# Two blocks on one core: four gate pairs by seven products, input normalised once, low parts by adding transfers, scales with 128-partition operands

## The chip, the cores and the metric

The kernel runs on one core of one Trainium2 chip, in one launch. The metric is device microseconds (us) of that core, as a median of runs. All numbers are fp32 on the outside; inside, a product of two fp32 matrices is made of three TensorE matmuls on rounded operands (type fp32r): high·high, high·low and low·high, where "high" is the rounded number and "low" is what rounding left.

## The reference, cut to what matters

The input x has 512 tokens of width 1024. A first block (normalisation, one wide projection, three branches, an output projection, a residual and a normalisation) feeds a second block. The change lies mostly in the second.

```python
def rmsnorm(x, g):
    y = xf * lax.rsqrt(jnp.mean(xf * xf, axis=-1, keepdims=True) + EPS)
    return (y * g).astype(x.dtype)
...
def first_block(...):
    h = rmsnorm(x, norm_g[l]); proj = h @ w_in[l]
    ...
    x = x + jnp.concatenate([y_a, y_b, y_c], axis=-1) @ w_out[l]
    return rmsnorm(x, final_norm_g)
...
def second_block(x, ...):
    p = h @ w_in[l] + b_in[l]
    a_u, a_v, q, k, v, r, a_low, g_a, g_b = split(p)
    y_a = spatial_gating(a_u, a_v, ...)          # gelu(a_u) * (mixed layer_norm(gelu(a_v)))
    o = gla_chunked(q, k, v, log_f)
    o = o * lax.rsqrt(jnp.mean(jnp.square(o), axis=-1, keepdims=True) + LN_EPS)
    y_b = o * gla_norm_g[l] * silu(r)
    m = sigmoid(g_a) * y_a + sigmoid(g_b) * y_b
    h = layer_norm(DEEPNORM_ALPHA * h + m @ w_out[l], ln1_g[l], ln1_b[l])
    f = jnp.square(relu(h @ w_ff1[l])) @ w_ff2[l]
    return layer_norm(DEEPNORM_ALPHA * h + f, ln2_g[l], ln2_b[l])
```

## The kernel before, in words

**A recorder and a planner.** The kernel does not issue instructions as it is written. Every call (`tt`, `act`, `mm`, a DMA) is recorded by `Recorder.add`, and at the end `rec.order` (L326) puts all instructions of the five queues (PE, ACT, DVE, POOL, SP) into an order by a list scheduler with a cost for each instruction; `rec.issue` (L484) emits that order. Each queue then runs in order. This is why every instruction stands at L502 in the profile. Buffers are bounded: 64 pages of 128x512 (`pg`), 8 PSUM banks (`ps`), 4 raw weight slots (`wr`), 4 slots each for high (`wh`, `fh`) and low (`wl`, `fl`) parts of weights.

**Weights.** Weights come as 184 chunks, mostly of 512 KB (128x1024). `load_to` (L631) loads a chunk into a raw slot by SP's queue; `split_to` (L639) calls `split` (L560): ACT copies to the rounded high part, DVE subtracts it from the raw chunk for the low part. `run_ahead` (L698) keeps it two chunks ahead.

**Feature-major units** (`unit_fm`, L727). One unit makes 128 output features of all 512 tokens: 8 slices of the inner dimension, three matmuls each, 24 matmuls of 512 columns. The second block has 40 such units in the order of `ORDER2` (L508): first `au0` to `au7`, then q, k, r, ga and gb. Each is evacuated from PSUM by a DVE multiplication with the page `rh` (the reciprocal root mean square of each token, spread over 128 partitions), and then by ACT. The operand hh/hl is thus the input without its per-token scale.

**Token-major units** (`units_tok`, L812). `av` (L1467 ff.) and `v` (L1530 ff.) have tokens on the partitions; a group of two chunks gives 96 matmuls of 256 or 260 columns. Order before: av, v, then the 40 units.

**Pairs** (`pair_weights` L731, `pair_fast` L765, `fast_operands` L793). In the first feed-forward matrix 11 pairs of units are made by seven products of half size (a Strassen-Winograd scheme): 7 x 4 x 3 = 84 matmuls of 256 columns in place of 48 of 512. Their weights are sums of chunks, made and split on DVE and ACT in advance; they take all four `wh`/`wl` slots (called `fh`/`fl` there). Four banks are combined by DVE and ACT.

**Scales and side work.** A scale by token is a column per tile of 128 tokens. `rsqrt_cols` (L868) makes the reciprocal root: square root on ACT, then five small DVE instructions. To spread it over partitions, `rows_of` (L881) transposes the columns to rows in a 64-partition tile `bhl`, and `bcast` (L891) multiplies a 64x128 selection (`sel`) with it, 128 columns at a time. `scale_page`, `mlstm_end`, `gla_end`, `mm_shift` and `ln1` use this; `gates` uses `sel` with 512 columns. Side work (`sg`, `gla`, `gla_end`, `resid`, ...) are generators in lanes which the units step.

Of the kernel before, what the change touches and what calls it, by code (L numbers as in the profile page):

```python
# [8 lines left out]
F32 = mybir.dt.float32  # L9
# [13 lines left out]
SLOT = 1088  # L23

# [145 lines left out]
class Recorder:  # L170
# [54 lines left out]
    def costs(self, o):  # L225
# [20 lines left out]
        elif eng == "DVE":  # L246
# [10 lines left out]
            elif o.what == "copy_predicated":  # L257
                o.cost = 160 + 1.1 * n
            elif o.what == "tensor_tensor_scan":
                o.cost = 1200  # L260
            elif n <= 16:
                o.cost = 165
        elif eng == "POOL":
            o.port = o.what != "memset"
            o.cost = 190 + 2.15 * n
# [94 lines left out]
    def schedule(self, caps, prio):  # L360
# [74 lines left out]
        while done < n:  # L435
# [11 lines left out]
            if e == "SP":  # L447
                b = o.kw["out"]
                size = 4.0 * 128 * (b.n if isinstance(b, View) else 512)
                wire = max(wire, s + 500) + size / 250.0  # L450
                o.end = max(wire, s + cost) + 1500
# [19 lines left out]
            for j in o.users:  # L471
                u = ops[j]
                u.ready = max(u.ready, o.end if u.eng != e else s + cost + (0 if e != "SP" else o.end - s - cost))
# [41 lines left out]
def tile_two_blocks(ctx, tc, wa, wb, xT, memT, vec, cst, rows, poolw, wst, wg2, out):  # L515
# [71 lines left out]
    sel = rec.tile(per, [64, 16], F32R, name="sel")  # L587
    selc = rec.tile(per, [128, 4, 4], F32R, name="selc")
    eps6 = rec.tile(per, [128, 1], F32, name="eps6")
    eps5 = rec.tile(per, [128, 1], F32, name="eps5")  # L590
    one1 = rec.tile(per, [128, 1], F32, name="one1")
    warm = rec.tile(per, [128, 1], F32, name="warm")
    rsm = rec.tile(per, [128, 24], F32, name="rsm")
    bhl = [rec.tile(per, [64, 128], F32R, name=f"bhl{i}") for i in range(2)]
# [6 lines left out]
    chunks = "b" * 4 + "a" * (4 + 4 + 8 + 2 + 2 + 2 + 2 + 4 + 12) + "a" * 12 + "a" * 8 + "b" * 8 + "a" * (8 + 32 + 8 + 32 + 32)  # L601
# [13 lines left out]
    fast_ff = set(range(FF1 + 4, FF1 + 4 + 2 * NFAST))  # L615

# [22 lines left out]
    def split_to(i):  # L639
        while n_sp[0] <= min(i, NCH - 1):  # L640
# [10 lines left out]
            else:  # L651
# [3 lines left out]
                split(h, l, t)  # L655
# [137 lines left out]
    def fast_operands(x, xh, xl):  # L793
# [3 lines left out]
        for kk in range(4):  # L797
            j = kk + 4
            for m, (t, s) in {1: (kk, L), 2: (j, L), 3: (j, R)}.items():
                b[m][0][kk], b[m][1][kk] = xh[t][:, s], xl[t][:, s]  # L800
            t56, t74 = pg(), pg()
            tt(V, t56[:, L], x[kk][:, R], x[kk][:, L], ALU.subtract)
            tt(V, t56[:, R], x[j][:, R], t56[:, L], ALU.subtract)
            tt(V, t74[:, L], x[j][:, R], x[kk][:, R], ALU.subtract)
            tt(V, t74[:, R], x[j][:, L], t56[:, R], ALU.subtract)
# [56 lines left out]
    def sqrt_of(v, n):  # L862
        t = small(16)[:, 0:n]
        act(t, v, ACTF.Sqrt)
        yield
        return t

    def rsqrt_cols(dst, v, n, t=None):  # L868

        if t is None:  # L870
            t = small(16)[:, 0:n]
            act(t, v, ACTF.Sqrt)
# [6 lines left out]
    bsel = [0]  # L879

    def rows_of(cols, n):  # L881

        p = bank()
        PE.transpose(out=p[0:n, 0:128], in_=cols, identity=ident)
        b = bhl[bsel[0] % 2]
        bsel[0] += 1
        act(b[0:n], p[0:n, 0:128], ACTF.Copy)
        tt(V, b[32:32 + n], p[0:n, 0:128], f(b[0:n]), ALU.subtract)
        return b

    def bcast(out, b, i):  # L891
        mm(out, sel[:, i:i + 1].to_broadcast([64, 128]), b, True, True)
# [6 lines left out]
    if True:  # L899
# [5 lines left out]
        V.memset(one1, 1.0)  # L905
        V.tensor_copy(out=onesr, in_=ones)
        for b in bhl:
            G.memset(f(b), 0.0)
# [16 lines left out]
        for k in range(8):  # L925
# [5 lines left out]
            split(w[1][:, s], w[2][:, s], w[0][:, s], eng=G)  # L931
        V.tensor_copy(out=sel, in_=ct[0:64, C_SEL:C_SEL + 16])
        V.tensor_copy(out=selc, in_=ct[:, C_SELC:C_SELC + 16].rearrange("p (h c) -> p h c", h=4))
# [22 lines left out]
    def scale_cols(dst, acc, nt, n, eps, p=None):  # L956
# [3 lines left out]
        rsqrt_cols(dst, v, nt)  # L960

    def scale_page(key, cols, nt):
        b = rows_of(cols, nt)
        yield
        p = bank()
        for j in range(nt):
            bcast(p[:, j * 128:(j + 1) * 128], b, j)
# [41 lines left out]
    def gates():  # L1009
# [4 lines left out]
        yield  # L1014
        ig, fg, ab, b, m, keep = [pg() for _ in range(6)]
# [7 lines left out]
        G.memset(f(ahl[0:64]), 0.0)  # L1023
# [31 lines left out]
        for h in range(4):  # L1055
            p = bank()
            mm(p, sel[:, h:h + 1].to_broadcast([64, 128]), ahl[0:64], True, True)
# [150 lines left out]
    def mlstm_end():  # L1208
# [9 lines left out]
        rsqrt_cols(c, v, 16)  # L1218
# [237 lines left out]
    del yh, yl, x2  # L1456
# [34 lines left out]
    def sg():  # L1491
# [3 lines left out]
        rsqrt_cols(rs, v, 4)  # L1495
# [31 lines left out]

# [790 lines left out]
```

## Time and profile before

| | us |
|---|---|
| median of three runs | 1118.11 (1118.07 to 1122.54) |
| the profiled execution: time | 1119.03 |
| the profiled execution: span from first to last instruction | 1117.3 |
| TensorE busy in that span | 1100.6 (99%), granted clock 0.996 on average |

The profile's busy time counts a matmul from its start to the end of its drain, and drains overlap the next matmul. A mean of 390 ns for a 512-column matmul is therefore not what it costs in a stream. The cost is the distance from one start to the next, which the timeline gives: the start of a merged row, its count, and the start of the next.

### The profile page before, as it was taken

The page shows a single profiled execution, that of the slowest core. Times are in us where ns is not written, and L with a number is a line of the kernel's source. Part 1 is how long each engine was busy: PE and PEld are TensorE (multiplying, and loading weights), DVE is VectorE, ACT ScalarE, POOL GpSimd, SP SyncE. Part 2 cuts the span into 40 slices and gives each one's busy share as a digit, 9 for nine tenths or more (in the row PEclk, how much of TensorE's full clock was granted, in tenths as well). Part 3 has the DMA queues.
Part 4 walks back from the last instruction along what each step waited for, and adds up shares of the span by engine and source line. Part 5 has one row for each costly group of instructions (what it writes and reads, how often), then busy time and mean ns, then how long its engine had stood idle before and what let it go on. Part 6 is the DMA issues. An engine that isn't in the chain of part 4 may idle for free.

```text
span 1117.3 us, 16271 instructions
## 1 busy us (share of the span) xinstructions
PE 1100.6 (99%) x6204; PEld 958.1 (86%) x6204; DVE 771.1 (69%) x1411; ACT 564.2 (50%) x964; POOL 182.7 (16%) x244
## 2 busy tenths in 40 slices
PE   7999999999999999999999999999999999999996
PEld 7888888878889999888888887899999988888885
DVE  6978888887336566667868876988898966233324
ACT  7766536444225343874655544446866666123301
POOL 5202101000012000253237550001000000000005
PEclk9999999999999999999999999999999999999998
DMA  8334322433322322232211132240133353244201
GB/s 303 114 104 148 108 76 67 151 101 108 95 94 92 101 76 76 78 94 85 84 57 57 57 98 72 89 139 1 61 111 114 114 171 96 91 132 133 75 1 76
DMA packets 33806, 108.94 MB, mean 98 GB/s; under 512 B 3888, under 2 KB 5040, under 8 KB 33728
## 3 DMA queue, kind: packets, MB, share of 16 engines
q1 hardware_dynamic: 33728, 107.90, 30.1%
q8 instruction: 49, 0.80, 0.3%
q14 instruction: 29, 0.24, 0.1%
HBM read 105.79 MB, written 2.10 MB: 97 GB/s over the span
## 4 chain that ended last, share of the span: by engine, by line
PE 96%; ACT 2%; DVE 1%; DMA 0%; issue 0%; SPq 0%; DVEq 0%
PE ps L502 96%; ACT pg L502 1%; DVE pg L502 1%; DVE wl L502 0%; DMA pg<-in_xT_dram 0%; ACT wh L502 0%; DVE sm L502 0%; SPq L502 0%; DVE sel L502 0%; DVE selc L502 0%; DVEq L502 0%
## 5 line engine op out<-in xcount | busy, mean ns | idle before, releaser
L502 PE MATMUL ps<-pg,wh 128*128 128x512 f32 (+1 forms) x1600 | 485.7, 386 | 0.0
L502 PEld LDWEIGHTS ps<-pg,wh 128*128 128x128 f32 x1600 | 294.4, 188 | 59.4 <-PE ps L502 0.7
L502 PE MATMUL ps<-pg,wl 128*128 128x512 f32 (+1 forms) x800 | 305.9, 383 | 0.0
L502 ACT ACTIVATE wh<-wr 128x1024 fp32r<-128x1024 f32 (+2 forms) x137 | 139.8, 1021 | 241.1 <-PE ps L502 209.0
L502 PE MATMUL ps<-pg,pg 128*128 128x512 f32 (+3 forms) x1264 | 236.5, 343 | 0.1
L502 ACT ACTIVATE pg<-pg 128x512 f32<-128x512 f32 (+7 forms) x328 | 174.2, 554 | 110.7 <-DVE pg L502 100.3
L502 PEld LDWEIGHTS ps<-pg,pg 128*128 128x128 f32 x1264 | 203.8, 191 | 28.8 <-ACT pg L502 0.6
L502 DVE TENSOR_TENSOR wl<-wr,wh 128x1024 fp32r<-128x1024 f32 (+1 forms) x129 | 165.0, 1282 | 76.8 <-ACT wh L502 76.3
L502 POOL TENSOR_TENSOR pg<-pg,pg 128x128 f32<-128x128 f32 (+4 forms) x113 | 109.3, 975 | 646.1 <-ACT pg L502 467.9
L502 PEld LDWEIGHTS ps<-pg,wl 128*128 128x128 f32 x800 | 150.2, 188 | 29.9
L502 PE MATMUL ps<-wh,pg 128*128 128x260 f32 (+2 forms) x800 | 168.1, 306 | 5.7 <-ACT wh L502 5.7
L502 DVE TENSOR_TENSOR pg<-pg,pg 128x512 fp32r<-128x512 f32 (+7 forms) x227 | 130.8, 603 | 23.1 <-ACT pg L502 14.9
L502 PEld LDWEIGHTS ps<-wh,pg 128*128 128x128 f32 x800 | 129.9, 190 | 12.6 <-ACT wh L502 5.7
L502 DVE TENSOR_TENSOR pg<-ps,pg 128x512 f32<-128x512 f32 (+4 forms) x128 | 80.4, 636 | 68.8 <-PE ps L502 65.3
L502 PE MATMUL ps<-wl,pg 128*128 128x260 f32 (+2 forms) x400 | 120.9, 304 | 0.1
L502 PE MATMUL ps<-pg,fh 128*128 128x256 f32 x616 | 105.4, 277 | 0.8 <-DVE pg L502 0.8
L502 PEld LDWEIGHTS ps<-pg,fh 128*128 128x128 f32 x616 | 91.8, 188 | 1.7 <-DVE pg L502 1.2
L502 DVE TENSOR_TENSOR pg<-wr,pg 128x512 fp32r<-128x512 f32 x62 | 40.7, 689 | 73.2 <-issue 45.0
L502 PE MATMUL ps<-pg,fl 128*128 128x256 f32 x308 | 81.6, 277 | 0.5 <-ACT pg L502 0.5
L502 PEld LDWEIGHTS ps<-wl,pg 128*128 128x128 f32 x400 | 75.8, 190 | 3.9 <-issue 0.5
L502 ACT ACTIVATE pg<-wr 128x512 fp32r<-128x512 f32 x62 | 35.4, 623 | 83.7 <-PE ps L502 75.2
L502 DVE SCALAR_TENSOR_TENSOR pg<-pg,pg 128x512 f32<-128x512 f32 (+4 forms) x76 | 54.7, 738 | 4.3 <-ACT pg L502 3.6
(148 smaller groups left out, 847.9 us busy)
## 6 DMA issues: line engine op xcount, KB each, us to landing
wr<-in_wa_dram SPq DMA_DIRECT2D x172, 512.0 KB, 3.6
wr<-in_wb_dram SPq DMA_DIRECT2D x10, 520.0 KB, 3.7
pg<-in_xT_dram SPq DMA_DIRECT2D x16, 256.0 KB, 4.3
pg<-in_rows_dram SPq DMA_DIRECT2D x10, 256.0 KB, 4.2
out_dram<-pg SPq DMA_DIRECT2D x8, 256.0 KB, 2.0
wr<-in_wb_dram SPq DMA_DIRECT2D x8, 130.0 KB, 4.3
pg<-in_memT_dram SPq DMA_DIRECT2D x4, 256.0 KB, 8.0
pg<-in_wst_dram SPq DMA_DIRECT2D x2, 256.0 KB, 4.5
```

What stands on the lines that cost most here:

```text
L502: getattr(real[o.eng], o.what)(**kw)
```

## The change

The order of the second block becomes av, au, v, then the other 32 units. Five edits:

1. The eight `au` units become four pairs by `fast_operands`, `pair_weights` and `pair_fast` (with `sums_of`, which adds hh and hl). The product with `mg` moves into a lane (`gate_au`).
2. After the second group of v, `normed` multiplies the eight pages of x2 by gain and `rh` and splits them; the 32 units that follow read this normalised input, and their evacuation no longer multiplies by `rh`. ACT reads PSUM itself. `resid` scales on ACT.
3. From the last two groups of v up to the first chunks of the output projection (chunks 76 to 116, 41 chunks), the low part is made by ACT as the negated high part, to which a DMA issued by GpSimd adds the chunk from HBM (`accum_op`).
4. `rows_of` puts each tile's row into its own 128 columns of a zeroed 128-partition page, and `bcast` multiplies a 128x128 operand (`selh`) with up to 512 columns at once. For up to four columns, `diag_of` and `spread` make two diagonal pages and multiply them by ones, without a transposition.
5. `rsqrt_cols` of up to four columns is one GpSimd power (exponent -0.5). The first chunks' low parts move from GpSimd to DVE, and the constants for `selh` and `selc` are made later, in `gates`.

The planner's cost figures get entries for the new instructions.

```diff
-    chunks = ... "a" * 12 + "a" * 8 + "b" * 8 + "a" * (8 + 32 + 8 + 32 + 32)
+    chunks = ... "a" * 12 + "a" * (8 + 8) + "b" * 8 + "a" * (32 + 8 + 32 + 32)
...
+    AU = 4 + len(ORDER1) + 12 + 8
+    fast_ff.update(range(AU, AU + 8))
+    acc = set(range(AU + 12, FF1))
...
-                split(h, l, t)
+                if c not in acc:
+                    split(h, l, t)
+                else:
+                    act(h, t, ACTF.Copy)
+                    act(l, t, ACTF.Copy, scale=-1.0)
+                    G.dma_start(out=l, in_=src[c], accum_op=ALU.add)
...
+    def rsqrt_cols(dst, v):
+        n = v.shape[1]
+        if n <= 4:
+            tt(G, dst, v, mhalf[:, 0:n], ALU.pow)
+            return
...
     def rows_of(cols, n):
+        tiles = min(n, 4)
         p = bank()
         PE.transpose(out=p[0:n, 0:128], in_=cols, identity=ident)
-        b = bhl[bsel[0] % 2]
-        bsel[0] += 1
-        act(b[0:n], p[0:n, 0:128], ACTF.Copy)
-        tt(V, b[32:32 + n], p[0:n, 0:128], f(b[0:n]), ALU.subtract)
+        b = pg(T, F32R)
+        G.memset(f(b), 0.0)
+        w = slice(0, tiles * 128)
+        m = pg()[0:n, w]
+        own = own16 if n == 16 else ident
+        tt(V, m.rearrange("p (j t) -> p j t", t=128), p[0:n, 0:128].unsqueeze(1).to_broadcast([n, tiles, 128]),
+           own[0:n, 0:tiles].unsqueeze(2).to_broadcast([n, tiles, 128]), ALU.mult)
+        act(b[0:n, w], m, ACTF.Copy)
+        tt(V, b[32:32 + n, w], m, f(b[0:n, w]), ALU.subtract)
         return b
-    def bcast(out, b, i):
-        mm(out, sel[:, i:i + 1].to_broadcast([64, 128]), b, True, True)
+    def diag_of(cols, n):
+        hi, lo = small(16, F32R)[:, 0:n], small(16)[:, 0:n]
+        act(hi, cols, ACTF.Copy)
+        tt(V, lo, cols, f(hi), ALU.subtract)
+        d = [pg(T, F32R), pg(T, F32R)]
+        for t, c in zip(d, (f(hi), lo)):
+            tt(V, t[:, 0:n * 128].rearrange("p (j t) -> p j t", t=128), ident.unsqueeze(1).to_broadcast([128, n, 128]),
+               c.unsqueeze(2).to_broadcast([128, n, 128]), ALU.mult)
+        return d
+    def spread(out, d):
+        w = out.shape[1]
+        mm(out, onesr, d[0][:, 0:w], True, False)
+        mm(out, onesr, d[1][:, 0:w], False, True)
+    def bcast(out, b, h=None, s=slice(0, T), start=True, stop=True):
+        h = 0 if h is None else h + 1
+        mm(out, selh[:, h * 128:(h + 1) * 128], b[:, s], start, stop)
+    def normed(raw, g, r):
+        for i, t in enumerate(raw):
+            stt(t, t, vc(g, i), r, ALU.mult, ALU.mult)
+            a, b = split_pg(t)
...
-            for j in range(4):
-                bcast(p[:, j * 128:(j + 1) * 128], b, 4 * j + h)
+            bcast(p, b, h)
...
+    hb = fast_operands(sums_of, hh, hl)
+    ulane = lane()
+    for i in range(0, 8, 2):
+        def evac(*cs):
+            for k, t in enumerate(cs):
+                tt(V, t, t, rh, ALU.mult)
+                act(t, t, ACTF.Gelu_apprx_tanh, bias=vc("b_au", i + k))
+                ulane.append(gate_au(i + k, t))
+        pair_fast(hb, evac)
+        for _ in range(2):
+            step(lanes)
...
+        if c == VN:
+            nh, nl = normed(x2, "final_norm_g", rh)
+    hh, hl = nh, nl
...
             t = pg()
-            tt(V, t, ps, rh, ALU.mult)
-            act(t, t, ACTF.Identity, scale=ISQ, bias=bqs[:, h:h + 1])
+            act(t, ps, ACTF.Identity, scale=ISQ, bias=bqs[:, h:h + 1])
...
     def mm_shift(m, hf):
-        for j in range(2):
-            o = hf.start + j * 128
-            mm(ps_h[m][:, o:o + 128], sel[:, o // 128:o // 128 + 1].to_broadcast([64, 128]), bmu, False, j == 1)
+        bcast(ps_h[m][:, hf], bmu, s=hf, start=False)
```

## Rows read from the trace of the kernel before

**Rows 1.** The page: busy time by engine; the chain that ended last.

```profile
PE 1100.6 (99%) x6204; PEld 958.1 (86%) x6204; DVE 771.1 (69%) x1411; ACT 564.2 (50%) x964; POOL 182.7 (16%) x244
PE 96%; ACT 2%; DVE 1%; DMA 0%; issue 0%; SPq 0%; DVEq 0%
```

**Rows 2.** Timeline of PE (start, us, instruction, count): a quiet stretch of 512 columns.

```profile
945.06 0.61 PE L502 MATMUL ps<-wh,pg 128*128 128x512 f32 x2
...
945.74 0.61 PE L502 MATMUL ps<-wh,pg 128*128 128x512 f32 x2
```

**Rows 3.** Stages (length; busy PE, PEld, DVE, ACT, POOL; clock, DMA share, GB/s).

```profile
339.40:385.40 46.00, 46.00 (x399) 45.78 (x398) 26.66 (x42) 19.09 (x31) 4.69 (x4) 1.00 0.30 94
385.40:439.90 54.50, 54.50 (x453) 53.54 (x452) 34.70 (x82) 21.86 (x35) 0.00 (x0) 1.00 0.26 78
487.00:735.00 248.00, 248.00 (x1181) 208.51 (x1180) 193.98 (x417) 125.66 (x225) 90.03 (x137) 1.00 0.25 79
735.00:792.00 57.00, 56.08 (x427) 53.07 (x426) 46.58 (x119) 34.05 (x78) 7.73 (x9) 0.97 0.16 53
792.00:901.50 109.50, 108.17 (x939) 107.12 (x939) 100.63 (x161) 76.79 (x124) 0.00 (x0) 1.00 0.33 105
```

**Rows 4.** Matmuls by shape: out<-in, rows, columns, count, busy us, mean ns.

```profile
L502 PE MATMUL ps<-pg,fh 128*128 128x256 f32 x616 | 105.4, 277 | 0.8 <-DVE pg L502 0.8
L502 PE MATMUL ps<-pg,fl 128*128 128x256 f32 x308 | 81.6, 277 | 0.5 <-ACT pg L502 0.5
L502 PE MATMUL ps<-bhl,sel 64*128 64x128 f32 x70 | 12.5, 287 | 0.0
```

**Rows 5.** Timeline of PE around 64-partition matmuls, four, two and two wide ones.

```profile
690.14 0.66 PE L502 MATMUL ps<-bhl,sel 64*128 64x128 f32 x4
690.73 0.73 PE L502 MATMUL ps<-pg,wh 128*128 128x512 f32 x2
...
693.70 0.66 PE L502 MATMUL ps<-bhl,sel 64*128 64x128 f32 x4
...
739.62 0.43 PE L502 MATMUL ps<-bhl,sel 64*128 64x128 f32 x2
739.98 1.70 PE L502 MATMUL ps<-pg,pg 128*128 128x256 f32 x12
741.61 0.43 PE L502 MATMUL ps<-bhl,sel 64*128 64x128 f32 x2
...
55.95 0.73 PE L502 MATMUL ps<-pg,sel 64*128 64x512 f32 x2
56.61 0.73 PE L502 MATMUL ps<-pg,wh 128*128 128x512 f32 x2
```

**Rows 6.** DVE and ACT groups by shape: count, busy us, mean ns, idle before.

```profile
L502 DVE TENSOR_TENSOR wl<-wr,wh 128x1024 fp32r<-128x1024 f32 x119 | 151.4, 1275 | 64.9 <-ACT wh L502 64.4
L502 DVE TENSOR_TENSOR pg<-ps,pg 128x512 f32<-128x512 f32 x95 | 65.4, 688 | 64.0 <-PE ps L502 62.1 <-POOL pg L502 1.5
L502 ACT ACTIVATE wh<-wr 128x1024 fp32r<-128x1024 f32 x119 | 125.8, 1058 | 223.7 <-PE ps L502 201.7 <-issue 20.7 <-DMA wr<-in_wa_dram 1.2
```

**Rows 7.** GpSimd groups by shape: the widest and one of the smallest.

```profile
L502 POOL TENSOR_TENSOR pg<-pg,pg 128x512 f32<-128x512 f32 x41 | 62.8, 1537 | 530.8 <-ACT pg L502 421.3 <-PE ps L502 98.6 <-DVE pg L502 9.3
L502 POOL TENSOR_TENSOR sm<-pg,sm 128x4 f32<-128x4 f32 x4 | 0.8, 202 | 0.3
```

**Rows 8.** DMA issues: count, KB each, median us from issue to landing.

```profile
wr<-in_wa_dram SPq DMA_DIRECT2D x172, 512.0 KB, 3.6
pg<-in_memT_dram SPq DMA_DIRECT2D x4, 256.0 KB, 8.0
```

**Rows 9.** Timeline of the last token tile's scale on DVE.

```profile
1109.66 0.22 DVE L502 TENSOR_SCALAR sm<-sm 128x1 f32<-128x1 f32 x2
...
1109.91 0.75 DVE L502 SCALAR_TENSOR_TENSOR pg<-ps,sm,pg 128x512 f32<-128x512 f32 x1
...
1111.53 0.75 DVE L502 SCALAR_TENSOR_TENSOR pg<-pg,sm,pg 128x512 f32<-128x512 f32 x1
```

More of the change, by code (lines that the diff above doesn't have):

```diff
@@ L262, in costs @@
                 o.cost = 165
+        elif eng == "POOL" and o.what == "dma_start":
+            o.cost = POOL_DMA
         elif eng == "POOL":
             o.port = o.what != "memset"
-            o.cost = 190 + 2.15 * n
+            o.cost = 190 + (235 if kw.get("op") == ALU.pow else 2.15) * n
             if o.what == "memset":
@@ L446, in schedule @@
                 cost += 1283
-            if e == "SP":
+            dma = o.what == "dma_start"
+            if dma:
                 b = o.kw["out"]
                 size = 4.0 * 128 * (b.n if isinstance(b, View) else 512)
-                wire = max(wire, s + 500) + size / 250.0
-                o.end = max(wire, s + cost) + 1500
+                wire = max(wire, s + 500) + size / (250.0 if e == "SP" else 170.0)
+                o.end = max(wire, s + cost) + (1500 if e == "SP" else 2500)
             else:
@@ L472, in schedule @@
                 u = ops[j]
-                u.ready = max(u.ready, o.end if u.eng != e else s + cost + (0 if e != "SP" else o.end - s - cost))
+                u.ready = max(u.ready, o.end if u.eng != e or dma else s + cost)
                 u.waiting -= 1
@@ L593, in tile_two_blocks @@
     rsm = rec.tile(per, [128, 24], F32, name="rsm")
-    bhl = [rec.tile(per, [64, 128], F32R, name=f"bhl{i}") for i in range(2)]
+    sums = rec.tile(per, [128, 5], F32, name="sums")
+    selh = rec.tile(per, [128, 5 * 128], F32R, name="selh")
+    own16 = rec.tile(per, [16, 4], F32, name="own16")
     ident = ct[:, C_ID:C_ID + 128]
@@ L959, in scale_cols @@
         ts(v, ps, 1.0 / n, eps, ALU.mult, ALU.add)
-        rsqrt_cols(dst, v, nt)
+        rsqrt_cols(dst, v)
     def scale_page(key, cols, nt):
-        b = rows_of(cols, nt)
+        b = diag_of(cols, nt)
         yield
         p = bank()
-        for j in range(nt):
-            bcast(p[:, j * 128:(j + 1) * 128], b, j)
+        spread(p[:, 0:128 * nt], b)
         r = pg(128 * nt)
@@ L1525, in tile_two_blocks, with sums_of, gate_au @@
     slane.append(sg())
+    def sums_of(t):
+        p = pg()
+        tt(V, p, f(hh[t]), f(hl[t]), ALU.add)
+        return p
+    def gate_au(i, t):
+        while ("sg", i) not in done:
+            yield
+        tt(V, mg[i], mg[i], t, ALU.mult)
+    hb = fast_operands(sums_of, hh, hl)
[9 more added lines that the diff above has]
+            step(lanes)
+    hb.clear()
     bvt = [pg(), pg()]
@@ L1779, in gla_end @@
             p = bank()
-            for j in range(4):
-                bcast(p[:, j * 128:(j + 1) * 128], b, 4 * j + h)
+            bcast(p, b, h)
             for w in range(2):
@@ L1820, in e, with fin_r @@
         def e(ps):
[L1821 to L1824 removed]
+            g = pg()
+            act(g, ps, ACTF.Tanh, scale=0.5, bias=half[:, 8 * n + i:8 * n + i + 1])
+            fin(i, ps, g)
         unit_fm(hh, hl, e)
[L1827 to L1828 removed]
+    def fin_r(i, ps, g):
+        t = pg()
+        act(t, ps, ACTF.Identity, bias=vc("b_r", i))
         stt(t, g, 1.0, t, ALU.add, ALU.mult)
@@ L1879, in tile_two_blocks @@
     }
-    for n, i in ORDER2:
+    for n, i in ORDER2[8:]:
         units[n](i)
@@ L1943, in ln1 @@
         ts(v, v, LN_EPS, None, ALU.add)
-        rsqrt_cols(mr[:, 0:2], v, 2, (yield from sqrt_of(v, 2)))
+        rsqrt_cols(mr[:, 0:2], v)
         stt(mr[:, 2:4], mr[:, 2:4], -1.0, mr[:, 0:2], ALU.mult, ALU.mult)
         yield
-        b = rows_of(mr[:, 0:4], 4)
+        b = diag_of(mr[:, 0:4], 4)
         yield
         pr = bank()
-        for j in range(4):
-            bcast(pr[:, j * 128:(j + 1) * 128], b, j)
+        spread(pr, b)
         for i in range(9):
@@ L1976, in tile_two_blocks @@
     p = bank()
-    for j in range(4):
-        bcast(p[:, j * 128:(j + 1) * 128], bmu, j)
+    bcast(p, bmu)
     for i in range(4):
```

95 lines of the change are left out of this document (37 added, 58 removed).

## The prediction, as it was made before the result was known

> **What bounds the kernel now.** I read the page first. TensorE (PE) is busy for 99% of the span and makes up 96% of the chain of work that ended last, while DVE is busy for 69%, ACT for 50% and GpSimd for 16% [rows 1]. The reader should take from this that what counts is the time that matmuls take up on PE, and that the other engines matter only where they make PE wait. A busy share can hide waits, since drains overlap, so I next took distances between starts from the timeline. Three 512-column matmuls (two shown, one left out between them) start within 0.68 us, 0.227 us each [rows 2]. Half of that, 0.1135 us, is the price of 256 columns in a stream. In the stage that already works with pairs, 924 matmuls of 256 columns [rows 4] take 109.5 us [rows 3], 0.1185 us each, so PE loses 4% there; DVE is busy for 100.63 of the 109.5 us, 92%. In the stretch 487 to 735, which holds nearly all the units after au, PE is busy throughout and DVE for 78% [rows 3]. So PE sets the pace, DVE is the next bound, and DVE is near to it where there are pairs.
>
> The sum is made against the profiled execution: 1119.03 us, with a span of 1117.3 and 1.7 us around it. The median is 1118.11, 0.9 us lower; I take the same difference off both.
>
> **Scales with 128 partitions: -12.1 us.** The trace shows 70 matmuls on 64 partitions with 128 columns [rows 4]: 13 groups of four and 9 of two. From one group of four to the next there are 3.56 us with 12 matmuls of 512 columns between them [rows 5]; 12 x 0.227 = 2.72, so a group costs 0.84 us on PE, though its columns are worth no more than 0.227. From one group of two to the next there are 1.99 us with 12 of 256 columns [rows 5], so a group costs 1.99 - 1.36 = 0.63 us. The new form has one ordinary matmul of the same columns. Nine groups of four (two branch ends and the mean's broadcast) save 9 x (0.84 - 0.227) = 5.5. Four others (rx, rh and twice ln1) become two matmuls by `spread`: 4 x (0.84 - 0.454) = 1.5. Eight groups of two in `mm_shift` save 8 x (0.63 - 0.114) = 4.1, and the one for the memory's scale 0.63 - 0.227 = 0.4. The two pairs of 512-column ones in `gates` take 0.66 us start to start [rows 5] against 0.454, plus a switch: 0.6 in all. The sum is 12.1, at a place where PE has no slack except around ln1. The bounds are 10 (the half of the `mm_shift` groups that lies over the wait for ln1 gives nothing) and 12.6 (five transposes that fall away too).
>
> **Four pairs: -3.8 us on PE.** Before, 8 x 24 = 192 matmuls of 512 columns take 192 x 0.227 = 43.6 us. After, 4 x 84 = 336 of 256 columns take 336 x 0.1185 = 39.8 at the pace of the present pairs, or 38.1 with no loss (-5.5).
>
> Here a rule speaks against the change. The row says that 256 columns cost 0.114 to 0.1185 us and 512 cost 0.227. The Trainium skill ("TensorE: Matmul & The Clock Gate", section "Back-to-back issue gap") gives a sustained 81 ns for 128 columns and 131 ns for 512; by that the units would take 25.2 us and the pairs at least 27.2, a loss. The trace does not agree in either figure, so the sum goes by the rows; the rule is kept as a rival below.
>
> **What DVE must do for it: +2 us.** A present pair costs DVE 100.63 / 11 = 9.15 us. The new ones add two multiplications by `rh` and two by `mg`, 4 x 0.69 [rows 6], 11.9 in all, where PE needs 9.5 to 10. Over the three stages av, au and v together: av and v hold 26.7 + 34.7 = 61.4 us of DVE now [rows 3]. Added are the operands (eight sums and eight splits at 0.69, sixteen differences of half width at an estimated 0.4: 17.4), the pairs 47.7 and `normed` (eight products, eight splits: 11.5); four low parts of 1.275 [rows 6] leave, 5.1. That is 132.9 us of DVE beside 46.0 + 39.8 + 54.5 = 140.3 of PE, 95%. At the 92% of the present pair stage it would take 144.5, 4.2 more than PE. The products by `mg`, 5.5, can be put off past v, and then nothing is lost. I take +2. The ends are 0 and, if nothing evens out between the stages, 4 x (11.9 / 0.92) - 39.8 = +11.9. Pages limit the evening out: x2 stays alive until `normed`, and hh, hl, the pairs' operands and av live beside it.
>
> **Later units: 0.** In 487 to 735 DVE is relieved of some 37 low parts of 1.275 and 32 products of 0.69, 69 us of its 194, and ACT gains 37 x 1.06 = 39 on 126 [rows 3, 6]. PE does not wait there now, so I count no gain (bound -2, in waits too short to be seen). PSUM banks are now freed by ACT alone, behind two weight copies; at 69% of ACT this stays hidden.
>
> **Adding transfers: 0 in the forecast.** No row shows a transfer issued by GpSimd or one that adds. The nearest rows are the loads of 512 KB by SP, 3.6 us to landing, and as the far end twice the slowest, 2 x 8.0 for 256 KB [rows 8]. I take a value near 3.6 to 6, as it moves the same bytes over the same engines. The waiting instruction stands in GpSimd's queue until ACT has made the negated part; behind it wait `gla`'s prefix sums, the new powers and `resid`, and for these ACT and DVE. GpSimd is busy for 90 of 248 us [rows 3], and 41 issues at 0.2 to 1.54 [rows 7] add 8 to 63. Hidden, unless the landing is later than the four slots allow (rival below). A second rule bears on this, and no run here shows it yet: by the Trainium skill ("DMA: Bandwidth & Descriptors", section "SWDGE vs HWDGE vs iDMA") GpSimd writes the descriptors of its transfers into SBUF, from which DVE can lock it out, while transfers of SP are immune. Its fit for such a transfer gives an estimate of 3.2 us for 512 KB, by which the term stays at 0.
>
> **Around ln1: +1 us.** In 735 to 792 PE is idle for 0.92 us and the granted clock is 0.97 [rows 3], 1.7 us lost. The chain to the spread scale loses five small DVE instructions and a transposition and gains two products of 0.69 per half. The power is unseen: GpSimd's rows give 0.2 for 128x4 and 1.54 for 128x512 [rows 7]; it has two elements per partition, so I take a value in the lower half. I take +1; ends -1.7 (the clock stays up) and +3.
>
> **End: -0.6 us; start: 0.** After the last matmul the reciprocal root ends the wait: the last-but-two product starts at 1111.53, though its other input is ready at 1109.91 + 0.75 = 1110.66 [rows 9]. With a power of at most 0.8 us 0.87 is won; with 1.54, 0.1. At the start, DVE takes eight low parts from GpSimd and gives up two constants: 0, within 1 either way.
>
> **Sum:** -12.1 - 3.8 + 2 + 0 + 1 - 0.6 = -13.5. 1119.03 - 13.5 = 1105.5, on the scale of the median 1104.6.
>
> **The rivals.**
> - *DVE bounds the pairs in full*: +11.9 in place of +2, -3.6 in all, 1114.5. For it: 11.9 us of DVE against 9.5 of PE a pair, and slots for only one pair at a time. Against it: 19 us of DVE idle in av, and 20 in v [rows 3].
> - *All goes well*: pairs without loss (-5.5), no lag, the clock stays up (-1.7), the short waits vanish (-2): about -21, 1097.
> - *The narrow matmul does not pay* (the page's rule): break-even is 43.6 / 336 = 0.13 us; at 0.15 the pairs take 50.4, 10.6 more than forecast, 1115. Against it: 924 such matmuls at 0.1185.
> - *Slower: the adding transfers come late.* A slot is free when its unit ends and is needed again three units later. Back to back units take 24 x 0.227 = 5.45 us, so a landing may take 16.3 - 2 x 1.06 = 14.2 us; with `gla` between them units take about 8 us (248 us for 31), and it may take 21.9. Beyond that PE waits: at 25 us a turn takes 25 + 2.1 + 8 = 35.1, 8.8 per unit, +0.8 x 37 = +28, 1133. For it: nothing measured; against it: 3.6 us for the same bytes, and 25% use of the DMA engines there.
>
> **How the numbers follow.** Forecast 0.56, DVE-bound pairs 0.15, all well 0.18, narrow matmul 0.04, late transfers 0.07. The forecast's own range is 1099 to 1110. The range 1096 to 1117 takes in the first four but for their tails. About 0.5%, 5.6 us, is what a measurement can tell from no change here. Below 1112.5 lie the forecast, the good case and a part of two others: 0.77. Within 0.5%: most of the DVE-bound case, 0.15. Slower: 0.08.
>
> **What would show it.** No 64-partition matmuls, and units that include a broadcast longer by 0.23 us rather than 0.84; four pairs in 40 to 42 us, with DVE over 90% busy; a landing under 14 us for the adding transfers; DVE near 50% in the later units; the last products right behind one another. It is wrong if PE shows idle time behind DVE in the au stage, or behind low parts in the units.

## The result and the profile after

The changed kernel takes 1106.28 us (median of 4 runs, 1106.04 to 1108.86) and the kernel before, measured beside it, 1119.06: a ratio of 0.9885, interval 0.9866 to 0.9904, some 12.9 us. The forecast was 1104.6. The profiled execution took 1106.5 us, with a span of 1104.8, 12.5 less than before. Of these 12.5 us, 1.7 are not work that was saved: the profile of the kernel before has a stretch of 3.4 us at a granted clock of 0.5 (1.2 GHz) at 763.0, right behind a wait of PE of 0.81 us, and the profile after has none before its tail.

The page and the stages of the kernel after, with the columns of [rows 1, 3]; the stages are av, the four pairs, v, the later units and the feed-forward pairs (FF1):

```profile
PE 1085.2 (98%) x6300; PEld 955.3 (86%) x6300; DVE 758.4 (69%) x1408; ACT 596.8 (54%) x1018; POOL 195.5 (18%) x280
...
336.40:381.90 45.50, 45.50 (x394) 45.41 (x393) 40.43 (x68) 22.92 (x39) 6.14 (x5) 1.00 0.21 66
381.90:431.60 49.70, 46.99 (x396) 45.43 (x396) 43.81 (x79) 28.65 (x41) 1.38 (x1) 1.00 0.27 91
431.60:478.80 47.20, 47.20 (x397) 47.20 (x398) 36.36 (x77) 25.41 (x39) 6.23 (x7) 1.00 0.76 188
478.80:720.00 241.20, 240.99 (x1129) 201.75 (x1128) 137.84 (x352) 166.94 (x286) 107.97 (x183) 1.00 0.70 157
778.90:890.00 111.10, 108.52 (x941) 107.39 (x939) 102.61 (x165) 78.30 (x132) 0.00 (x0) 1.00 0.34 112
```

PE's busy time fell by 15.4 us. In the later units DVE is down from 78% to 57% and ACT up from 51% to 69%, in the direction forecast (DVE near 50% was said); PE is busy throughout them, before and after. So nothing in this stage shows what the adding transfers are good for; that takes experiments.

Three views answer to steps of the prediction. First the timeline of PE after: two broadcasts in the later units (ends of a stretch of 12 matmuls of 512 columns), then two of `mm_shift`:

```profile
685.13 0.39 PE L507 MATMUL ps<-pg,selh 128*128 128x512 f32 x1
...
688.10 0.39 PE L507 MATMUL ps<-pg,selh 128*128 128x512 f32 x1
...
733.83 0.28 PE L507 MATMUL ps<-pg,selh 128*128 128x256 f32 x1
...
735.38 0.28 PE L507 MATMUL ps<-pg,selh 128*128 128x256 f32 x1
```

From broadcast to broadcast are 2.97 us; less 12 x 0.227 this leaves 0.25, where the kernel before paid 0.84. In `mm_shift` the period is 1.55 instead of 1.99 [rows 5].

Second, the DMA queues (packets, MB, share of the 16 engines) and the issues (count, KB, median us to landing):

```profile
q1 hardware_dynamic: 33728, 107.90, 29.8%
q0 software_dynamic: 5904, 21.53, 11.2%
...
wr<-in_wa_dram SPq DMA_DIRECT2D x172, 512.0 KB, 3.7
wl<-in_wa_dram POOLq DMA_DIRECT2D x37, 512.0 KB, 7.2
```

An adding transfer lands after 7.2 us. That is over the 3.6 to 6 that I took and far under the 14.2 at which it would have delayed units.

Third, the power in ln1 (GpSimd) and the power and last products of the tail:

```profile
745.19 0.72 POOL L507 TENSOR_TENSOR sm<-sm,mhalf 128x2 f32<-128x2 f32 x1 [8.60 <-DVE sm L507]
...
1098.41 0.55 POOL L507 TENSOR_TENSOR sm<-sm,mhalf 128x1 f32<-128x1 f32 x1 [0.52 <-DVE sm L507]
1098.43 0.75 DVE L507 SCALAR_TENSOR_TENSOR pg<-ps,sm,pg 128x512 f32<-128x512 f32 x1
1099.30 0.75 DVE L507 SCALAR_TENSOR_TENSOR pg<-pg,sm,pg 128x512 f32<-128x512 f32 x1
```

The second product starts 0.12 us after the first ends; it was 0.87 [rows 9].

One sign that the prediction named for being wrong did show, once: PE idle behind DVE in the stage of the four pairs. At its end PE waits for a low part of v's weights:

```profile
431.42 0.39 PE L507 MATMUL ps<-wl,pg 128*128 128x260 f32 x1 [1.71 <-DVE wl L507]
```

### The profile page after: what moved, and what is told of

Read it like the earlier page. It is cut to its first block, busy times and chain, and to the rows that moved or that the text cites. A ratio compares the mean times of both kernels' runs of the same rounds, so it can differ in the third digit from the quotient of the medians.

```text
span 1104.8 us, 16591 instructions
## 1 busy us (share of the span) xinstructions
PE 1085.2 (98%) x6300; PEld 955.3 (86%) x6300; DVE 758.4 (69%) x1408; ACT 596.8 (54%) x1018; POOL 195.5 (18%) x280
## 3 DMA queue, kind: packets, MB, share of 16 engines
q1 hardware_dynamic: 33728, 107.90, 29.8%
q0 software_dynamic: 5904, 21.53, 11.2%
## 4 chain that ended last, share of the span: by engine, by line
PE 95%; ACT 2%; DVE 2%; DMA 1%; issue 0%; SPq 0%; DVEq 0%; ACTq 0%
PE ps L507 95%; ACT pg L507 2%; DVE pg L507 1%; DMA wl<-in_wa_dram 1%; DMA wr<-in_wb_dram 0%; ACT L507 0%; DVE wl L507 0%; DVE sm L507 0%; DVE fl L507 0%; ACT wl L507 0%; SPq L507 0%; ACT wh L507 0%; DVE big L507 0%; DVEq L507 0%; ACTq L507 0%
## 5 line engine op out<-in xcount | busy, mean ns | idle before, releaser
L507 PE MATMUL ps<-pg,wh 128*128 128x512 f32 (+1 forms) x1472 | 445.6, 384 | 0.0
L507 PEld LDWEIGHTS ps<-pg,wh 128*128 128x128 f32 x1472 | 271.4, 188 | 53.2 <-issue 0.4
L507 PE MATMUL ps<-pg,wl 128*128 128x512 f32 (+1 forms) x736 | 281.6, 383 | 0.2 <-DMA wl<-in_wa_dram 0.2
L507 DVE TENSOR_TENSOR pg<-pg,pg 128x512 fp32r<-128x512 f32 (+8 forms) x274 | 161.8, 615 | 44.9 <-ACT pg L507 27.2
L507 PE MATMUL ps<-pg,fh 128*128 128x256 f32 x840 | 146.3, 280 | 2.2 <-ACT pg L507 1.5
L507 DVE TENSOR_TENSOR wl<-wr,wh 128x1024 fp32r<-128x1024 f32 (+2 forms) x88 | 103.3, 1179 | 53.4 <-ACT wh L507 52.2
L507 PEld LDWEIGHTS ps<-pg,fh 128*128 128x128 f32 x840 | 125.6, 188 | 4.5 <-ACT pg L507 2.1
L507 PE MATMUL ps<-pg,fl 128*128 128x256 f32 x420 | 111.4, 277 | 1.4 <-DVE fl L507 1.4
L507 PEld LDWEIGHTS ps<-pg,fl 128*128 128x128 f32 x420 | 77.0, 188 | 1.6 <-DVE fl L507 1.6
L507 DVE TENSOR_TENSOR pg<-ps,pg 128x512 f32<-128x512 f32 (+6 forms) x92 | 55.7, 615 | 24.3 <-PE ps L507 17.4
```

The source lines that it names most:

```text
L507: getattr(real[o.eng], o.what)(**kw)
```

## The experiments

All ratios are to the kernel before, run beside the kernel on the same chip; us are the ratio's distance from 1, times 1119.

**The price of 64 partitions.** The kernel before, all its 64-partition operands padded with zeros to 128, with the same 74 matmuls (its main lines; `gates` and `mm_shift` are padded alike):

```diff
-    sel = rec.tile(per, [64, 16], F32R, name="sel")
+    sel = rec.tile(per, [128, 16], F32R, name="sel")
-    bhl = [rec.tile(per, [64, 128], F32R, name=f"bhl{i}") for i in range(2)]
+    bhl = [rec.tile(per, [128, 128], F32R, name=f"bhl{i}") for i in range(2)]
-        mm(out, sel[:, i:i + 1].to_broadcast([64, 128]), b, True, True)
+        mm(out, sel[:, i:i + 1].to_broadcast([128, 128]), b, True, True)
...
```

> The kernel before, with one thing changed: bhl, sel and the operand of gates have 128 partitions (the added ones zero), the matmuls stay 70 of 128 columns and 4 of 512. Theory (what costs is the change between 64 and 128 partitions): a group of four falls from 0.84 to 4 x 0.11 = 0.44 us, a group of two from 0.63 to 0.22, those of gates by 0.4; 13 x 0.40 + 9 x 0.41 + 0.8 = 9.7 us less, about 1109.4. Rival (what costs is the number of small matmuls, whatever their rows): nothing changes, 1118 to 1119.

Measured: 1112.37 us, ratio 0.9925 (0.99 to 0.995), -8.4 us, for 9.7 expected. Its PE timeline, two groups of four with 12 matmuls of 512 columns between them, then two groups of two in `mm_shift`:

```profile
684.77 0.56 PE L502 MATMUL ps<-bhl,sel 128*128 128x128 f32 x4
...
687.97 0.56 PE L502 MATMUL ps<-bhl,sel 128*128 128x128 f32 x4
...
736.04 0.33 PE L502 MATMUL ps<-bhl,sel 128*128 128x128 f32 x2
736.21 1.65 PE L502 MATMUL ps<-pg,pg 128*128 128x256 f32 x12
737.70 0.33 PE L502 MATMUL ps<-bhl,sel 128*128 128x128 f32 x2
```

With the matmuls unchanged in number and columns, the period of a group of two falls from 1.99 to 1.66 us, and that of a group of four from 3.56 to 3.20. A group gives back much the same, 0.33 and 0.36, with two matmuls or with four, so the price goes by the group and not by the matmul: it is the change from 128 to 64 partitions and back that costs. There are 24 such groups, and 24 x 0.34 = 8.2 us agrees with the 8.4. One wider matmul in place of two (1.55) adds another 0.11 in `mm_shift`; in place of four (2.97) it adds 0.23. The Trainium skill ("TensorEngine Tiling (Array Packing)", section "Key Properties") says that a change of tiling mode drains TensorE; this run agrees and gives it a price, some 0.34 us for a change there and back.

**The scales alone.** The kernel before with the whole new form of the scales (`diag_of`, `spread`, the wide `rows_of`, `selh`), with the old reciprocal roots:

> The kernel before with the new scales alone: selh, rows_of, diag_of, spread and bcast of the changed kernel, the old reciprocal root, the old order, no pairs for au, no adding transfers, no normed. Theory: 12.1 us less, 1107, so that nearly all of the measured gain is here. Rival (the gain is spread over the edits, and the pairs carry 4 to 5 of it): 7 to 8 us less, 1111.

Measured: 1120.16 us, ratio 0.9993 (0.9978 to 1.0007), no gain; theory and rival both missed. PE loses it again between the mean and the end of the FF1 pairs. Here are its timelines of DVE, ACT and PE in that stretch, followed by the one row of the padded kernel that answers to its first three:

```profile
732.80 0.68 DVE L502 TENSOR_TENSOR pg<-ps,ct 4x512 f32<-4x512 f32 x1 [0.16 <-PE ps L502]
...
733.51 0.63 ACT L502 ACTIVATE pg<-pg 4x512 fp32r<-4x512 f32 x1 [2.26 <-DVE pg L502]
...
734.71 0.68 DVE L502 TENSOR_TENSOR pg<-pg,pg 4x512 fp32r<-4x512 f32 x1
...
740.82 0.39 PE L502 MATMUL ps<-pg,wl 128*128 128x256 f32 x1 [0.52 <-DVE pg L502]
...
742.08 1.29 DVE L502 TENSOR_TENSOR pg<-wr,pg 128x512 fp32r<-128x512 f32 x2
...
745.65 1.81 PE L502 MATMUL ps<-pg,pg 128*128 128x256 f32 x13 [0.52 <-DVE pg L502]
...
755.13 1.01 PE L502 MATMUL ps<-pg,onesr 128*128 128x512 f32 x2 [0.69 <-DVE pg L502]
...
757.75 0.69 PE L502 MATMUL ps<-ct,pg 128*128 128x128 f32 x2 [1.60 <-ACT pg L502]
```

```profile
733.67 0.28 DVE L502 TENSOR_TENSOR bhl<-ps,bhl 4x128 fp32r<-4x128 f32 x1
```

One broadcast's operand costs DVE 2 x 0.68 = 1.36 us where the old row cost 0.28. DVE has the low parts of the last weights to make in the same stretch (742.08), and PE waits for it. The first pair starts later for it, at 787.0 for 784.2. The windows of mean to pairs and of the pairs, of this kernel, then of the padded one:

```profile
732.50:787.00 54.50, 51.03 (x400) 49.08 (x397) 45.08 (x116) 32.70 (x72) 7.86 (x9) 0.97 0.14 40
787.00:903.60 116.60, 111.59 (x939) 109.34 (x940) 103.95 (x170) 77.57 (x131) 0.00 (x0) 1.00 0.31 108
```

```profile
732.60:784.20 51.60, 50.34 (x421) 49.46 (x419) 45.66 (x118) 33.80 (x78) 7.74 (x9) 1.00 0.19 58
784.20:895.70 111.50, 110.19 (x939) 109.16 (x939) 100.66 (x161) 77.11 (x124) 0.00 (x0) 1.00 0.31 105
```

Of the 2.9 us in the first window, 1.7 are a fall of the granted clock to 0.5 for 3.4 us at 757.8, behind the waits of 0.69 and 1.60 us shown above. The same pairs take 5.1 us more. By pairs, 2.3 of them lie in the first two, where PE waits 1.2 us for a weight part `fl` from DVE; 1.1 in the third to fifth, which run at the slower pace of the last section; and 2.2 in the last five, with the sixth 0.5 shorter. The last five take 10.3 us each, for 9.9 in the padded kernel and 9.5 in the kernel before, each with one wait. One such wait, PE and then ACT:

```profile
867.34 0.39 PE L502 MATMUL ps<-pg,fh 128*128 128x256 f32 x2
868.21 0.39 PE L502 MATMUL ps<-pg,fl 128*128 128x256 f32 x1 [0.47 <-ACT pg L502]
```

```profile
867.77 0.38 ACT L502 ACTIVATE pg<-ps 128x256 f32<-128x256 f32 x1 [0.58 <-PE ps L502]
```

It is a handshake. ACT's copy out of a bank waits for PE, and PE's next matmul waits for the copy, which ends at 868.15; the detour costs 0.64 us against a matmul right behind, and such a pair is 0.77 us longer than one at 9.52. By the program's order I take it for a copy of one half of `p16` (one of the four banks of a pair) that the planner put ahead of the last matmuls into the other half; the trace shows only who waits for whom. DVE then waits 0.80 us for PE in the same pair, so it is not full either. The pairs stage of the kernel before has 2 stalls of this size (0.6 to 0.7 us), that of this kernel 7; two of these are waits for DVE's part of the same evacuation.

**au as eight units.** The changed kernel with au as eight units instead of four pairs, at the new place:

> The changed kernel with au as eight units again, in the new place ahead of v, all else kept. Theory (pairs save 3.8 to 5.5 us of PE and give most of it back waiting for DVE): 1 to 2 us more than the changed kernel, 1107.5 to 1108.3. Rival A (DVE's lag costs nothing): 5.5 more, 1111.8. Rival B (the pairs cost more than they save): at or below 1106.

Measured: 1110.69 us, ratio 0.9908 (0.9886 to 0.993), 2.6 us more than the changed kernel's 0.9885. From the first matmul of av to the last of v it takes 144.0 us to the changed kernel's 142.2, 1.8 us more, and the five other traces with pairs there lie at 142.1 to 142.4. By whole times alone the two intervals overlap, and five of its FF1 pairs ran 0.37 us slower each (the pace described in the last section), which lies outside these stages. So the pairs pay, narrowly, by the stage.

**Without the adding transfers.** The changed kernel with `acc = set()`:

> The changed kernel with no adding transfers: the 41 low parts are made by DVE again, all else kept. Theory (PE did not wait for DVE there before, so its relief hides): within 1 us of the changed kernel, 1105.3 to 1107.3, though DVE goes back from 57% to near 79% busy in the later units. Rival (the relief is what keeps PE fed after the pairs, above all in v): 3 to 6 us more.

Measured: 1114.79 us, ratio 0.9951 (0.9931 to 0.9972), 7.4 us more than the changed kernel. My expectation of no effect falls; the rival had the sign, and its +3 to +6 is within what the intervals allow. Most of the loss shows again from the mean to the end of the pairs: 167.8 us to the changed kernel's 160.9, with 8 stalls of the handshake's size in the pairs.

**Without the powers.** The changed kernel with square root and reciprocal everywhere:

```diff
-        if n <= 4:
-            tt(G, dst, v, mhalf[:, 0:n], ALU.pow)
-            return
```

> The changed kernel with one part undone: every reciprocal root is again ACT's square root with five small DVE instructions; nothing on GpSimd. Theory (in the scales-alone run the gain was lost between the mean and the end of the first feed-forward pairs, where a longer chain at ln1 leaves DVE behind and the pairs, at DVE's limit, never catch up): the pairs show a stall of some 0.6 us each again and the time is 1111 to 1116, +5 to +10 on the changed kernel's 1106.3. Rival (the prediction's own terms: some 0.3 to 0.8 us for each of two halves of ln1, 0.6 at the end): 1107 to 1108.5. Second rival (the order that the planner happens to choose): anywhere within some 5 us either way, without more stalls in the pairs.

Measured: 1109.6 us, ratio 0.9903 (0.9878 to 0.9929), 2.0 us more than the changed kernel, with intervals that overlap. The traces say where: PE waits 1.60 us in ln1, where the changed kernel waits 0.18, and the end is 0.8 us longer. The pairs are not longer, with 2 stalls. So the power's terms were about as priced, and my theory that the powers save the pairs falls.

**Scales and powers.**

> The kernel before with two parts of the change: all scales with 128 partitions, as in the scales-alone run, and the powers on GpSimd for the reciprocal roots of up to four columns (the last tile's stays as it was). Theory (the power keeps ln1's chain short, so DVE enters the pairs without debt): the stretch from the mean to the first pair loses some 4 us rather than 8.9, and the time is 1107 to 1110, 8 to 12 under before. Rival (it is the low parts on DVE in the later units that leave it behind, which the adding transfers relieve): 1115 to 1120.

Measured: 1118.9 us, ratio 0.9981 (0.9968 to 0.9994), -2.1 us. The stretch to the pairs is 1.4 us shorter than with the scales alone, the pairs as long (116.7, 7 stalls). The rival's range holds: ln1's chain is not what loses the gain.

**Other orders of the same instructions.** Every edit makes the planner write a new order. Three of its figures (two costs of GpSimd, the rate of loads) were moved by 2 to 6 per cent, in the scales-alone kernel (shown) and likewise in the changed one:

```diff
-            o.cost = 190 + 2.15 * n
+            o.cost = 200 + 2.2 * n
-                wire = max(wire, s + 500) + size / 250.0
+                wire = max(wire, s + 500) + size / 235.0
```

> The scales-alone kernel, the same instructions, with two costs of the planner changed by 2 to 6 per cent (an element on GpSimd 2.2 ns for 2.15, a base of 200 for 190, loads at 235 for 250 bytes per ns), so that it writes out another order. Theory (the loss of the scales-alone kernel comes from DVE's limit, not from its order): 1117 to 1121 again, with the stalls in the pairs. Rival (the order's luck): 1107 to 1114, since the 12 us of PE time that the scales give back are there in any order.

> The changed kernel, the same instructions, with the same two costs of the planner changed as in the replanned scales-alone kernel. If orders of equal merit differ by little: 1104 to 1109. If the order's luck is worth as much as a part of the change: 1110 to 1116, or under 1103.

Measured: 1119.78 us, ratio 0.9999 (0.9986 to 1.0013), and 1108.6 us, 0.9894 (0.9875 to 0.9912). Both came out as expected: the scales alone bring nothing in either order, with 7 stalls again, and the changed kernel keeps its gain within 1 us.

**Scales with adding transfers, and adding transfers alone**, each on the kernel before (the planner also gets cost figures for the new transfers, left out here):

```diff
+    acc = set(range(4 + len(ORDER1) + 12 + 16 + 8, FF1))
...
-                split(h, l, t)
+                if c not in acc:
+                    split(h, l, t)
+                else:
+                    act(h, t, ACTF.Copy)
+                    act(l, t, ACTF.Copy, scale=-1.0)
+                    G.dma_start(out=l, in_=src[c], accum_op=ALU.add)
...
```

> The kernel before with two parts of the change: all scales with 128 partitions, as in the scales-alone run, and the later weights' low parts (37 of them) by adding transfers from GpSimd; no powers, no pairs for au, no normed input. Theory (the new operands cost DVE 1.4 us where the old row cost 0.3, and only where DVE is relieved of low parts does it still reach the first feed-forward pair with five parts of its weights ready, so that the 12 us of the scales are kept): five low parts fl ready at the first pair, the stretch from the mean to that pair losing about 4 us for 8.9, and 1107 to 1111. Rival (the loss of the scales-alone kernel is not DVE's debt from low parts): 1116 to 1121.

> The kernel before with one part of the change: 37 later weights' low parts by adding transfers; the scales stay on 64 partitions. Theory (the adding transfers give no PE time of their own; they only keep DVE ahead, and in the kernel before it is ahead already, with five parts ready at the first feed-forward pair): 1117 to 1121, within 3 us of the kernel before. Rival (they are worth some 7 to 10 us by themselves, as the runs without and with them suggest): 1110 to 1114.

Measured: both together 1110.92 us, ratio 0.9908 (0.9879 to 0.9938), -10.3 us; adding alone 1120.78 us, ratio 1.0 (0.9984 to 1.0017). That is the core of this case: two parts that bring 0.8 and 0 us each bring 10.3 together. Mean to pairs and pairs, of the kernel with both:

```profile
729.80:783.00 53.20, 50.30 (x403) 48.19 (x401) 44.34 (x117) 33.62 (x76) 7.29 (x9) 1.00 0.11 39
783.00:891.80 108.80, 107.81 (x942) 107.10 (x941) 100.59 (x163) 76.37 (x124) 0.00 (x0) 1.00 0.33 105
```

The pairs are back to 108.8 us, with 2 stalls and no wait for `fl`. The number of weight parts `fl` that DVE has begun by the first pair (window; DVE busy and count) was my measure of its lead. Scales alone, then with adding:

```profile
700.00:787.00 87.00, 3.79 (x4) 0.98 0.23 74
```

```profile
700.00:783.00 83.00, 4.53 (x5) 1.00 0.36 99
```

The lead is there as expected: the first of these parts is begun 53.9 us ahead of the first pair, where the scales alone begin it 9.7 us ahead. The stretch before the pairs, though, is only 1.3 us shorter, and that is less than the 1.7 of the fall of the clock that the scales alone have in it; ln1's long chain stays, with its wait of 1.60 us. The profiled execution of both is the shortest of its four runs (1108.98 to 1113.88 us), so the ratio is the better measure of their gain.

With adding alone the stretch before the pairs is 2.5 us shorter than in the kernel before, but 1.7 of this is the fall of the clock at 763.0 that the kernel before has in it. The pairs take 112.7 us, 3.2 more, with 7 stalls, 5 more than before at 0.64 each. So adding alone wins little ahead of the pairs and loses 3.2 us by their order.

**au's products on GpSimd**, alone and together with the start's eight low parts on GpSimd as before:

```diff
-        tt(V, mg[i], mg[i], t, ALU.mult)
+        tt(G, mg[i], mg[i], t, ALU.mult)
-                tt(V, t, t, rh, ALU.mult)
+                tt(G, t, t, rh, ALU.mult)
```

> The changed kernel with the products of the au pairs by rh and by mg on GpSimd, which is busy there for 1.4 of 49.7 us, rather than on DVE. Theory (the 4.3 us that the av, au and v stages take over 92.6 are DVE's, as the prediction's surplus says): the three stages take 2 to 3 us less, 1103 to 1104.5 for 1106.3. Rival (it is the pace of the 256-column matmuls there and a single late weight part, 1.7 us, that more time on DVE doesn't mend): 1106 to 1107.5.

> The changed kernel with the au products on GpSimd and, besides, the eight low parts of the start on GpSimd again as in the kernel before, where the last matmul of the first unit came 1.2 us earlier. If both hold: 1102 to 1103.5, 0.5 to 1.2 under the run with the au products alone; if neither: 1106 to 1107.5.

Measured: 1106.52 us, ratio 0.9866 (0.9844 to 0.9888), and 1106.95 us, 0.9878 (0.985 to 0.9906). Against the changed kernel's 0.9885 neither can be told apart, and both lie where the rival put them. av to the end of v takes 142.4 us in both where the changed kernel takes 142.2. But the run did not relieve DVE by much. The 16 products are gone from DVE, 11.0 us, yet DVE's busy time in the three stages falls only from 120.6 to 117.7 us, since other DVE instructions ran longer. One group of low parts, with the products on GpSimd and then in the changed kernel:

```profile
L507 DVE TENSOR_TENSOR wl<-wr,wh 128x1040 fp32r<-128x1040 f32 x4 | 7.2, 1869 | 0.0
```

```profile
L507 DVE TENSOR_TENSOR wl<-wr,wh 128x1040 fp32r<-128x1040 f32 x4 | 4.8, 1237 | 1.0 <-issue 1.0
```

Of these four the last, with no product of GpSimd beside it, takes 1.23 us. The other three each start while such a product runs, end 1.10 us after that product's end, and take up to 2.32. So the runs do not show whether DVE's share of these stages is what costs there. No kernel here is measurably better than the changed one.

## Why the prediction was right, and where it was not

Where the profiled executions spent their time, in us from the first matmul of each stage to that of the next:

| stretch | before | scales alone | adding alone | both | changed |
|---|---|---|---|---|---|
| start to av | 339.4 | 336.2 | 340.1 | 336.1 | 336.4 |
| av to the end of the later units | 332.5 | 333.8 | 334.1 | 332.2 | 331.2 |
| to the mean | 63.9 | 62.5 | 63.9 | 61.5 | 61.5 |
| to the first FF1 pair | 56.2 | 54.5 | 53.7 | 53.2 | 49.8 |
| FF1 pairs | 109.5 | 116.6 | 112.7 | 108.8 | 111.1 |
| to the end of the span | 215.8 | 215.4 | 215.5 | 215.5 | 214.8 |
| span | 1117.3 | 1119.0 | 1120.0 | 1107.3 | 1104.8 |

Falls of the granted clock to 0.5 for 3.4 us, worth 1.6 to 1.7 us each, lie in the second row of scales alone and of adding alone, and in the fourth row (to the first FF1 pair) of before and of scales alone (columns of [rows 3]; these two, in this order):

```profile
763.00:766.40 3.40, 3.40 (x18) 3.40 (x18) 3.33 (x10) 2.71 (x7) 1.20 (x2) 0.51 0.02 5
```

```profile
757.80:761.20 3.40, 3.40 (x16) 3.24 (x17) 3.33 (x11) 3.19 (x7) 0.73 (x1) 0.50 0.00 0
```

The kernel with both and the changed one have none in any row but the last. The two of the fourth row follow a wait of PE in ln1 (0.81 and 1.60 us); the kernel with both has the same wait of 1.60 and no fall, so the wait alone does not bring it about.

The sum of -13.5 came out at -12.5 in the profiled executions, 1.7 of it the clock. By its terms:

- *Scales, -12.1.* Measured -10.0 (span of the kernel with both), 1.7 of it the clock, and -10.3 by the ratio, and only beside the adding transfers. The price of a group was right: 0.84 fell to 0.25 and 1.99 to 1.55. What was wrong is the sentence that PE has no slack at this place except around ln1 (what PE won there it lost again by waits and a slower pace up to the end of the FF1 pairs), and the count of the new operands on DVE. I counted them around ln1, five small instructions against two products, and not the two of 0.68 for each broadcast row.
- *Later units 0, adding transfers 0.* This step failed. I looked for their worth in waits of PE in their own stage, found none, and priced them at nothing. Their worth lies 100 us later, in the stretch from the mean to the end of the FF1 pairs: 9.5 us beside the scales (-10.3 to -0.8), 7.4 in the changed kernel, and in the kernel before nothing. In the traces of scales alone and of both, the pairs differ by 7.8 us: 4.1 in the last five, each of which has a handshake in the one and none in the other; 3.1 in the first two, where the wait for `fl` lies; and 0.7 in the four between, which differ in the pace of the last section. The two errors cancel, since both parts are in the change; the total was right for a partly wrong reason.
- *Four pairs, -3.8 on PE and +2 for DVE, -1.8.* The run with eight units gives -1.8 in the stages concerned. The stages took 142.2 us to the 142.3 of the sum (140.3 + 2). Of the +2, the wait of 1.71 us for DVE's low part can be seen, and two waits for ACT of 0.5 each besides. Whether DVE's busy share, 88% in the pairs' stage, is behind them is not shown, as the run that was to relieve DVE hardly did. The rival in which DVE bounds the pairs in full is out. "40 to 42 us with DVE over 90%" can't be read off, as the planner put other units' matmuls between the pairs (396 in the 49.7 us, where the pairs have 336).
- *The narrow matmul.* It pays: 256 columns cost 0.113 to 0.118 us here too. The two sustained figures of the Trainium skill ("TensorE: Matmul & The Clock Gate", section "Back-to-back issue gap") would have it at a loss; the trace agrees with neither.
- *Adding transfers late.* Out: 7.2 us to landing. The estimate of 3.2 from the fit in the Trainium skill ("DMA: Bandwidth & Descriptors", section "Anatomy of one DMA — SWDGE (gpsimd) path") is under half of that. DVE was 57% busy in this stage; whether it held GpSimd's descriptors up, no run here tells apart from the price of adding.
- *ln1, +1.* With the power at 0.72 us, in the lower half as taken, PE waits 0.18 us in ln1, and the clock stays at 1.00 in this stretch of the profiled run. So the +1 did not come, and the 1.7 of the clock did, as only the good case had it. The powers are worth 2.0 us in all by the medians, of which I had 0.6 (the end). The end itself gave 1.0: from the last matmul to the end of the span 9.0 us became 8.0.

What stays open is why the planner puts the handshakes in. They come in the four kernels that have the new scales without adding, whose DVE has at most four parts done at the first pair, where the others have five; but they come with adding alone too, at five parts. A replanned order of the scales-alone kernel had all 7 again, so they are no accident of one order; a plan that forbids them was not tried, and adding alone and both were not replanned. This matters for the core of the case. The scales alone and adding alone each have five pairs more with a handshake than both, 5 x 0.77 = 3.9 us. If an order without them gave this back (an estimate), the two parts alone would bring some 4.7 and 3.9 us by the ratios, of the 10.3 that they bring together, or 3.9 and 1.2 of 8.3 by the traces without the falls of the clock: more than half. That they bring more together than apart, as built, is measured; how much of it is DVE's lead and how much the planner's order is not shown.

Not tried alone were the normalised input, ACT's part in the evacuations, and the moved low parts of the start. The step from both (span 1107.3) to the changed kernel (1104.8) holds them together with the four pairs and the powers.

## What to carry to other kernels

Here the relief of an engine that made nobody wait was worth nothing by itself, and 7 to 10 us beside an edit that loads the same engine. So price edits that load and edits that relieve one engine as a pair, and look for the bill in the stage where this engine is nearest to its limit (and there in the order, too), not where the edit is. Before a new form of an operand, count its instructions on every engine: the zero-padded rows won 8.4 us with seven edited lines and no load on DVE, while the form that saves more PE time needed the adding transfers beside it. When parts of a change come out right only in total, undo them one at a time and in pairs, since single runs of two parts that need each other show nothing of either. When a planner rewrites the order with every edit, replan each of these kernels too. And before two profiles are compared stage by stage, look where each has its falls of the clock: one is as large as a small part of a change.

## What the runs showed of the hardware

**A stream of 256-column matmuls has two paces.** It is fast at 0.1134 us and slow at 0.1178, 4% apart, with the granted clock at 1.00, PE busy throughout and no wait in either. The changed kernel and its replanned twin, with the same instructions, in the same window of the FF1 pairs:

```profile
845.00:888.00 43.00, 43.00 (x380) 42.85 (x379) 39.90 (x64) 29.38 (x47) 0.00 (x0) 1.00 0.34 114
```

```profile
845.00:888.00 43.00, 43.00 (x368) 43.00 (x367) 38.59 (x61) 28.34 (x46) 0.00 (x0) 1.00 0.31 110
```

43 us hold 380 matmuls in the one and 368 in the other. The pace holds for tens of us and changes at some interruptions. In the changed kernel's first pair (triples of matmuls on PE):

```profile
382.06 0.40 PE L507 MATMUL ps<-pg,fh 128*128 128x256 f32 x2
...
383.11 0.40 PE L507 MATMUL ps<-pg,fh 128*128 128x256 f32 x2
...
384.51 0.50 PE L507 MATMUL ps<-pg,fh 128*128 128x256 f32 x2 [0.53 <-ACT pg L507]
...
384.98 0.39 PE L507 MATMUL ps<-pg,fh 128*128 128x256 f32 x2
...
392.80 0.39 PE L507 MATMUL ps<-pg,fh 128*128 128x256 f32 x2
```

Ahead of the wait three triples take 1.05 us, 0.117 each matmul; behind it 23 triples take 7.82, 0.113 each. A pair of 84 matmuls takes 9.52 or 9.89 us by this, and the last five pairs of a kernel up to 1.9 us more or less. What chooses the pace wasn't found. The 0.1185 that I took as what DVE costs in the present pairs was misread: in the kernel before, eight of the eleven pairs take 9.52 us, 0.113 a matmul. The rest lies in the first, second and sixth pair (10.6, 12.4 and 10.5 us): 16 matmuls of 128 columns there are not the pairs' own (1.8 us), two stalls cost 1.3, and the sixth pair runs in part at the slow pace.

**Adding by DMA takes the engines nearly twice as long.** Per MB the queue of GpSimd, which holds the adding transfers alone, takes 11.2% / 21.53 = 0.52% of the engines' time and that of SP 29.8% / 107.90 = 0.28%, and 512 KB land after 7.2 us for 3.7. How much of this is the adding and how much the issue by GpSimd, no run here tells apart.

**A GpSimd product stretches DVE's instructions beside it.** A low part of 128x1040 took DVE 1.23 us alone and up to 2.32 us when it started while GpSimd multiplied pages of 128x512 (the run with au's products on GpSimd), and the two products beside two such low parts took 2.28 us each, where those just before had taken 1.28. Moving work from DVE to GpSimd there gave back 2.9 of 11.0 us.
